# Two pools of six 8 KB tiles in place of one pool of twelve, in a two-layer decoder trunk

## The chip, the cores and the metric

One core of a Trainium2 chip runs the whole kernel. The metric is the device time of one execution in microseconds (us). The engines are named as in the profile: PE (TensorE; PEld are its weight loads), DVE (VectorE), ACT (ScalarE), POOL (GpSimd) and SP (SyncE, which here only issues DMAs). Each engine works through its own queue strictly in the order in which the program was written out for it.

## What is computed

Two layers, each with four sub-layers on x of 512 tokens by 1024 columns, everything in float32. The part that matters here is the SwiGLU, which stands twice in each layer:

```python
def swiglu(x, w_in, w_out):
    gate, up = jnp.split(x @ w_in, 2, axis=-1)
    return (jax.nn.silu(gate) * up) @ w_out

for l in range(DEPTH):                       # DEPTH = 2, D_FF = 2816
    x = x + 0.5 * rms_norm(swiglu(rms_norm(x, ln_ffn1_pre[l]), w_ffn1_in[l], w_ffn1_out[l]), ln_ffn1_post[l])
    x = x + rms_norm(token_mixing(...), ln_mix_post[l])
    x = x + 0.5 * rms_norm(swiglu(rms_norm(x, ln_ffn2_pre[l]), w_ffn2_in[l], w_ffn2_out[l]), ln_ffn2_post[l])
    gate = jax.nn.sigmoid(rms_norm(x, ln_ple_pre[l]) @ w_ple_gate[l])
    x = x + rms_norm(gate * (p[l] @ w_ple_proj[l]), ln_ple_post[l])
```

## The kernel before

**Precision.** A float32 operand is split into a high part (a rounding copy, on ACT, line 139) and a low part (the rest, on DVE or POOL, line 140), and a product is three matmuls: high by high (L167), high by low (L168) and low by high (L169). So each weight tile is loaded by a DMA into a raw tile and must pass through ACT and then DVE before PE can use it.

**A SwiGLU's first half** (`ffn`) is a loop over 22 *units*, one for each block of 128 hidden columns. A unit multiplies by a scheme of seven products instead of eight (block sums of the weights and of x take the place of the eighth); a product is 4 x 3 matmuls of 128x256, so a unit has 84. What a unit needs, in the code's names: the raw weights `wr` (two DMAs of 512 KB, `ffn_load`, L316); the split `w12` of their first half, for the products `gate` starts with (bank `p12`); block sums `sx` and `sy` (DVE, L355, L357, L358) and their splits `w75` and `w63`; and the split `u2` (also printed as `w4`) of a quarter. DVE then puts the banks together (L367, L370, L372, L374, L375, L378), ACT applies silu (L376), and DVE writes the product into the hidden tile `h` (L382). One `h` tile holds four units, so a new one is asked for in units 0, 4, 8, 12, 16 and 20.

**The second half** (`ffn_out`) runs in two passes over the output's halves (h = 0 and 1). A pass takes *P blocks* (plain: 48 matmuls) and *S blocks* (the seven-product scheme, for two hidden blocks at once) in the order of `FSEQ`: P0 S3 S4 P1 S5 S6 P2 S7 S8 S9 in the first pass, S6 S7 S8 S9 S3 S4 S5 in the second. A tail of plain blocks (10 in the first pass; 0, 1, 2 and 10 in the second) is multiplied token block by token block, and after each token block `finish` empties its banks with the help of the tile `us` (DVE, L497). An S block's weights come by DMA into `ws_r` (L440), get three sums on DVE (L442 to L444) and a split `wb`; the hidden tiles get theirs as `hq`, which stay from their P block to the end of the second pass.

**The slots.** All these tiles, and others, are 8 KB per partition, and they come from one pool, `slots`, by `slot()`: one tag, "s", with twelve buffers (`NS`). They are: `xr` (x kept for later sums), three `tx` (sums of x for products 4, 6 and 7, alive for the whole first half), `wr`, `h`, `hq`, `ws_r`, `us`, the splits of the second pass's tail weights, `wor`/`wot` of the mixing's output product, and `pT`/`wpg` of the last sub-layer. The pool is closed during the token mixing and opened again after it.

**What sets the order.** The program is written for a framework that schedules it before it runs: it takes the instructions by the order of the source, gives each tile a buffer of its tag when its turn comes, estimates times, and writes a fixed queue for each engine. Tiles of one tag are given out in the order in which the source asks for them: a tile cannot get a buffer before every tile that was asked for earlier with that tag has been given one, even while buffers are free. In the source, the `h` tile of unit 4 is asked for at the end of unit 4's body, ahead of the `wr` of unit 5. What the scheduler sets is the order in the queues; on the chip an instruction waits only for its own semaphores and for what stands ahead of it in its engine's queue.

Of the kernel before, what the change touches and what calls it, by code (L numbers as in the profile page):

```python
# [9 lines left out]
F32 = mybir.dt.float32  # L10
F32R = mybir.dt.float32r
# [9 lines left out]
NM = DFF // 128  # L21
EPS = 1e-6
SLOT = 2048
NS, NW = 12, 3
G = 4
BANKS = {"m": 2, "r": 3}
MAINL, AUXL = "mmoa", "brrr"
# [45 lines left out]
class Trunk:  # L73
# [35 lines left out]
    def close_slots(self):  # L109
        self.slots_pool.__exit__(None, None, None)  # L110

    def slot(self, shape, name, dt=F32):
        assert np.prod(shape) <= SLOT
        return self.slots.tile([128] + list(shape), dt, tag="s", name=name, bufs=NS)

    def pl_(self, i):
        return self.nc.gpsimd if PL[i] == "1" else self.nc.vector
# [33 lines left out]
    def wblock(self, ap, name, slot=False, raw=None, eng=None):  # L151

        c = ap.shape[1]
        if raw is None:
            raw = self.wraw.tile([128, c], F32, tag="raw", name=name + "_r")
        self.nc.sync.dma_start(out=raw, in_=ap)
        if slot:
            w = self.slot([2, c], name, F32R)
            self.split(w[:, 0], w[:, 1], raw, eng)
            w = w[:, 0], w[:, 1]  # L160
        else:
            w = self.wsplit(raw, name, eng)
        return [self.cut(w, slice(i * c // 2, (i + 1) * c // 2)) for i in range(2)]
# [46 lines left out]
    def turn(self, t, xn, ffn):  # L210
        nc = self.nc
        v_, a_, g_ = nc.vector, nc.scalar, nc.gpsimd
        ps = []
        for j in range(2):
            p = self.aux_tile("xtp").rearrange("p (a b) -> p a b", a=4)
            for i in range(4):
                k = 4 * j + i
                nc.tensor.transpose(p[:, i], xn[:, k * 128:(k + 1) * 128], self.ident)
            ps.append(p)
        kss = [slice(0, 4), slice(4, 8)]  # L220
        ts = slice(t * 128, (t + 1) * 128)
        if ffn and t == 0:
            self.xr = self.slot([2, 8, 128], "xr")
        if ffn and t == 2:
            self.tx = [self.slot([2, 4, 256], "tx", F32R) for _ in range(3)]
        if not ffn or t < 2:
            for p, ks in zip(ps, kss):
                self.split(self.xh[:, ks, ts], self.xl[:, ks, ts], p)
                if ffn:
                    a_.activation(self.xr[:, t, ks], p, AF.Copy)  # L230
            return
        EB, E1, E3, E4 = None, g_, g_, g_

        u = t - 2
        xr = self.xr
        t2, t3 = (self.tmp.tile([128, 4, 128], F32, tag="tb0", name="tx", bufs=4) for _ in range(2))
        t1, t4 = (xr[:, u, ks] for ks in kss)
        a_.activation(t3, ps[0], AF.Copy)
        v_.tensor_tensor(t1, t1, ps[0], ALU.subtract)
        v_.scalar_tensor_tensor(t2, ps[1], -1.0, t1, ALU.mult, ALU.subtract)  # L240
        v_.tensor_tensor(t3, ps[1], t3, ALU.subtract)
        g_.tensor_tensor(t4, t4, t2, ALU.add)
        self.split(self.xh[:, kss[1], ts], self.xl[:, kss[1], ts], ps[1], EB)
        us = slice(u * 128, u * 128 + 128)
        self.split(self.xh[:, kss[0], ts], self.xl[:, kss[0], ts], t1, E1)
        for q, x, e in zip(self.tx, (t2, t3, t4), (None, E3, E4)):
            self.split(q[:, 0, :, us], q[:, 1, :, us], x, e)
# [14 lines left out]
    def out_proj(self, nb, part, blocks, gain, scale, after, tail):  # L262

        half0 = []
        for h in range(2):
            ps = [self.mm_tile("y0") if h == 0 else self.aux_tile("y1") for _ in range(NT)]
            cut = nb - (tail if h else 1)

            def one(i, w, a, t):
                for j in range(2):  # L270
                    self.mm3(ps[t], [q[:, t * 128:(t + 1) * 128] for q in a[j]], w[j],
                             i == 0 and j == 0, i == nb - 1 and j == 1)

            for i in range(cut):
                w, a = self.wblock(blocks(h, i), "wo", eng=self.nc.gpsimd if h == 0 and OW[i] == "1" else None), part(h, i)
                for t in range(NT):
                    one(i, w, a, t)
            raws = [None] * nb
            if h and tail == nb:
                raws = [q[:, j] for q in [self.slot([2, 1024], "wor") for _ in range(nb // 2)] for j in range(2)]  # L280
            rest = [(i, self.wblock(blocks(h, i), "wot", bool(h), raws[i], self.nc.gpsimd if (raws[i] is not None and OE[i] == "1" if h else OW[i] == "1") else None), part(h, i)) for i in range(cut, nb)]
            def finish(t):
                e = self.out_evac(ps[t], gain, h, scale)
                if h == 0:
                    half0.append(e)
                else:
                    self.postnorm(t, half0[t], e, scale)
                    self.late.append(after(t))

            for t in range(NT):  # L290
                for i, w, a in rest:
                    one(i, w, a, t)
                if t:
                    finish(t - 1)
                if h and t > 1:
                    self.flush(1)
            self.ending(h, finish)
# [12 lines left out]
                f()  # L310

    def ffn_load(self, l, w, ms):
        rs = [self.slot([2, 1024], "wr") for m in ms]
        for i in range(2):
            for m, r in zip(ms, rs):
                self.nc.sync.dma_start(out=r[:, i], in_=self.ins[f"w_ffn{w}_in"][l, m, i])  # L316
        return rs
# [6 lines left out]
    def ffn(self, l, w, after):  # L324
# [11 lines left out]
        hs = []  # L336
# [16 lines left out]
        def unit(m, r, pa, a):  # L353
            sx, sy = (self.wraw.tile([128, 1024], F32, tag="raw", name="ws") for _ in range(2))
            v_.tensor_tensor(sx.rearrange("p (i c) -> p i c", i=2), r[:, :, lo],  # L355
                             r[:, 1].rearrange("p (i c) -> p i c", i=2), ALU.add)
            v_.tensor_tensor(sy[:, lo], sx[:, hi], r[:, 0, lo], ALU.add)  # L357
            v_.tensor_tensor(sy[:, hi], sy[:, lo], r[:, 0, hi], ALU.add)  # L358
            sx, sy = self.wsplit(sx, "w75"), self.wsplit(sy, "w63")
            u2 = [self.tmp.tile([128, 512], F32R, tag="sg", name="w4") for _ in range(2)]  # L360
            self.split(u2[0], u2[1], r[:, 1, hi])
            pc, pb, pd = self.aux_tile("p63"), self.aux_tile("p75"), self.mm_tile("p4")
            b = self.tmp.tile([128, S], F32, tag="tb1", name="up", bufs=2)

            P, Q = (L, H) if m % 2 else (H, L)
            product(6, self.cut(sy, lo), pc[:, L])
            v_.tensor_tensor(a[:, Q], pc[:, L], a[:, P], ALU.add)  # L367
            product(7, self.cut(sx, lo), pb[:, P])
            product(5, self.cut(sx, hi), pb[:, Q])
            v_.tensor_tensor(b.rearrange("p (i t) -> p i t", i=2), pb.rearrange("p (i t) -> p i t", i=2),  # L370
                             a[:, None, Q].to_broadcast([128, 2, 256]), ALU.add)
            v_.tensor_tensor(a[:, P], pa[:, H], a[:, P], ALU.add)  # L372
            product(3, self.cut(sy, hi), pc[:, H])
            v_.tensor_tensor(a[:, Q], pc[:, H], b[:, Q], ALU.add)  # L374
            v_.tensor_tensor(b[:, Q], pb[:, Q], b[:, P], ALU.add)  # L375
            a_.activation(a, a, AF.Silu)  # L376
            product(4, u2, pd[:, L])
            v_.tensor_tensor(b[:, P], b[:, P], pd[:, L], ALU.subtract)  # L378
            if m % 4 == 0:
                hs.append(self.slot([8, 256], "h"))  # L380

            v_.scalar_tensor_tensor(hs[m // 4][:, m % 4 * 2:m % 4 * 2 + 2], b.rearrange("p (i t) -> p i t", i=2), -1.0,  # L382
                                    a.rearrange("p (i t) -> p i t", i=2), ALU.mult, ALU.mult)
# [15 lines left out]
    def ffn_out(self, hs, blocks, gain, scale, after):  # L399
# [12 lines left out]
        def plain(h, b, slot=False):  # L412
            w = self.wblock(blocks(h, b), "wo", slot)
            if b not in kept:
                q = self.slot([2, 4, 256], "hq", F32R)
                self.split(q[:, 0], q[:, 1], raw(b))
                kept[b] = q
            return w, kept[b]
# [17 lines left out]

        def right(ap):

            r = self.slot([8, 256], "ws_r")
            nc.sync.dma_start(out=r[:, 0:4].rearrange("p i d -> p (i d)"), in_=ap)  # L440

            v_.tensor_tensor(r[:, 4:6], r[:, 1:4:2], r[:, 0:1].to_broadcast([128, 2, 256]), ALU.add)  # L442
# [7 lines left out]
        for h in range(2):  # L450
# [32 lines left out]
                        for u in range(2):  # L483
                            add(n, u, A[n], B[n], b == sb[-1] and n not in (2, 3, 4))
            rest = [plain(h, b, bool(h)) for b in tail]
            us = self.slot([4, 512], "us")
            u1, u2, u3, u4 = (us[:, i].rearrange("p (u d) -> p u d", u=2) for i in range(4))
            a_.activation(u1, banks[1], AF.Copy)
            v_.tensor_tensor(u2, banks[6], u1, ALU.add)
# [1024 lines left out]
```

## Time and profile before

| | us |
|---|---|
| median of three runs | 2292.49 (2291.95 to 2295.7) |
| the profiled execution, device time | 2293.78 |
| its span in the trace | 2292.1 |
| PE busy | 2154.4 (94%) |
| DVE busy | 1735.3 (76%) |
| ACT busy | 1006.8 (44%) |
| POOL busy | 330.7 (14%) |

The profiled execution took 1.7 us more than its span, and 1.3 us more than the median. The four first halves of the SwiGLUs end, by the trace, near 283, 969, 1420 and 2102 us. In the trace's rows, a wait is given in brackets behind the instruction that came after it, with the instruction that ended it. The start column is in us from the span's start. A matmul's duration overlaps the next one's: the pace of PE is the distance from start to start.

### The profile page before, as it was taken

What the parts mean: (1) busy time and instruction counts of PE and PEld (TensorE: products, weight loads), DVE (VectorE), ACT (ScalarE), POOL (GpSimd) and SP (SyncE); (2) the same over time, 40 slices, a digit from 0 to 9 for tenths busy, and PEclk for the clock granted to TensorE, in tenths of its full rate; (3) what the DMA queues carried; (4) which work ended last, traced back from release to release, by engine and by line L of the source; (5) the groups of instructions that cost most, each with busy time, mean ns of one, the idle gap of its engine ahead of it and who ended that gap; (6) DMA issues with size and microseconds to landing.
All of it is one profiled execution on the core that took longest, in us unless ns stands there. A gap on an engine that the chain in (4) does not pass through costs nothing.

```text
span 2292.1 us, 39759 instructions
## 1 busy us (share of the span) xinstructions
PE 2154.4 (94%) x16256; PEld 1991.3 (87%) x16256; DVE 1735.3 (76%) x2886; ACT 1006.8 (44%) x1653; POOL 330.7 (14%) x424
## 2 busy tenths in 40 slices
PE   5999999999988999999979999999999989999998
PEld 5998999888767998999879899998887789899996
DVE  8988886555768888886688888775557698888774
ACT  4343433446545443433554344344464454344343
POOL 4000001132234000002330000111322330000111
PEclk9999999999999999999989999999999999999999
DMA  5222123322032222123322122243220322122232
GB/s 211 93 74 75 65 83 129 124 74 56 20 146 94 93 74 74 65 83 129 138 111 86 62 84 70 78 142 121 61 60 12 147 111 93 56 92 74 90 115 73
DMA packets 67495, 208.61 MB, mean 91 GB/s; under 512 B 15728, under 2 KB 16752, under 8 KB 67312
## 3 DMA queue, kind: packets, MB, share of 16 engines
q1 hardware_dynamic: 67312, 206.07, 25.5%
q8 instruction: 127, 2.08, 0.4%
q14 instruction: 56, 0.46, 0.1%
HBM read 199.23 MB, written 6.82 MB: 90 GB/s over the span
## 4 chain that ended last, share of the span: by engine, by line
PE 74%; DVE 12%; ACT 5%; DMA 3%; issue 3%; POOL 1%; SPq 0%; ACTq 0%; DVEq 0%; POOLq 0%
PE y L463 14%; PE p L169 12%; PE p L167 12%; PE p L168 12%; DVE w L140 2%; PE pkrv L169 1%; PE pkrv L168 1%; PE pkrv L167 1%; DVE xn L207 1%; PE y L169 1%; PE y L168 1%; PE y L167 1%; ACT w L139 1%; PE pgt L167 1%; PE pgt L168 1%
## 5 line engine op out<-in xcount | busy, mean ns | idle before, releaser
L167 PE MATMUL p<-xh,w 128*128 128x256 f32 x1408 | 415.9, 296 | 50.7 <-ACT w L139 46.3
L169 PE MATMUL p<-xh,w 128*128 128x256 f32 x1408 | 415.5, 295 | 9.8 <-POOL w L140 6.4
L168 PE MATMUL p<-xl,w 128*128 128x256 f32 x1408 | 411.6, 293 | 0.2 <-DVE xl L140 0.2
L167 PEld LDWEIGHTS p<-xh,w 128*128 128x128 f32 x1408 | 283.4, 202 | 57.0 <-ACT w L139 50.4
L167 PE MATMUL p<-tx,w 128*128 128x256 f32 x1056 | 301.3, 289 | 15.5 <-ACT tx L139 11.7
L168 PE MATMUL p<-tx,w 128*128 128x256 f32 x1056 | 296.8, 284 | 6.5 <-DVE tx L140 6.5
L169 PEld LDWEIGHTS p<-xh,w 128*128 128x128 f32 x1408 | 283.5, 201 | 15.1 <-DVE w L140 8.1
L169 PE MATMUL p<-tx,w 128*128 128x256 f32 x1056 | 293.3, 284 | 2.9 <-DVE w L140 2.9
L139 ACT ACTIVATE w<-ws 128x1024 fp32r<-128x1024 f32 x176 | 186.1, 1057 | 244.1 <-PE p L169 139.3
L168 PEld LDWEIGHTS p<-xl,w 128*128 128x128 f32 x1408 | 283.3, 201 | 0.9 <-DVE xl L140 0.8
L140 DVE TENSOR_TENSOR w<-ws,w 128x1024 fp32r<-128x1024 f32 x176 | 221.6, 1259 | 49.9 <-ACT w L139 46.9
L167 PEld LDWEIGHTS p<-tx,w 128*128 128x128 f32 x1056 | 202.8, 192 | 23.7 <-ACT tx L139 13.0
L168 PEld LDWEIGHTS p<-tx,w 128*128 128x128 f32 x1056 | 203.5, 193 | 7.6 <-DVE tx L140 7.6
L169 PEld LDWEIGHTS p<-tx,w 128*128 128x128 f32 x1056 | 199.7, 192 | 3.3 <-DVE w L140 3.2
L499 POOL TENSOR_TENSOR tb<-tb,ln_ffn_post 128x512 f32<-128x512 f32 x16 | 27.2, 1700 | 1192.6 <-ACT junk L196 1192.3
L463 PE MATMUL y<-wo,hq 128*128 128x256 f32 x1536 | 190.5, 282 | 0.0
L463 PEld LDWEIGHTS y<-wo,hq 128*128 128x128 f32 x1536 | 185.2, 190 | 0.4
L139 ACT ACTIVATE w<-wr 128x512 fp32r<-128x512 f32 (+1 forms) x176 | 144.2, 839 | 62.5 <-PE p L169 22.1
L463 PE MATMUL y<-ws_r,h 128*128 128x256 f32 x672 | 158.2, 379 | 0.0
L140 DVE TENSOR_TENSOR w<-wr,w 128x512 fp32r<-128x512 f32 (+1 forms) x161 | 152.4, 947 | 0.8 <-ACT w L139 0.7
L463 PEld LDWEIGHTS y<-ws_r,h 128*128 128x128 f32 x672 | 121.3, 190 | 13.4
L376 ACT ACTIVATE gate<-gate 128x512 f32<-128x512 f32 x88 | 54.9, 624 | 142.5 <-DVE gate L374 142.4
(426 smaller groups left out, 4745.7 us busy)
## 6 DMA issues: line engine op xcount, KB each, us to landing
wr<-in_w_ffn_in SPq DMA_DIRECT2D x176, 512.0 KB, 4.2
ws_r<-in_w_ffn_out SPq DMA_DIRECT2D x56, 512.0 KB, 3.7
wo_r<-in_w_ffn_out SPq DMA_DIRECT2D x32, 512.0 KB, 3.2
pkrv_r<-in_w_rw SPq DMA_DIRECT2D x16, 512.0 KB, 3.7
wpg_r<-in_w_ple_gate SPq DMA_DIRECT2D x16, 512.0 KB, 4.2
xd<-x SPq DMA_DIRECT2D x8, 512.0 KB, 3.1
x<-xd SPq DMA_DIRECT2D x8, 512.0 KB, 3.3
pq_r<-in_w_q SPq DMA_DIRECT2D x8, 512.0 KB, 3.5
```

The lines of the kernel that those rows point to most:

```text
L139: self.nc.scalar.activation(hi, src, AF.Copy)
L140: (eng or self.nc.vector).tensor_tensor(lo, src, hi.bitcast(F32), ALU.subtract)
L167: mm(out, a[0], b[0], start=first, stop=False)
L168: mm(out, a[0], b[1], start=False, stop=False)
L169: mm(out, a[1], b[0], start=False, stop=last)
L207: v_.scalar_tensor_tensor(xn[:, h], self.x[:, t, h], r, gain[:, h], ALU.mult, ALU.mult)
L376: a_.activation(a, a, AF.Silu)
L463: nc.tensor.matmul(banks[n][:, u], x, y, start=n not in seen, stop=last and i == len(todo) - 1, skip_group_check=True)
L499: (g_ if not h or QL[0] == "1" else v_).tensor_tensor(tb, tb, gain[:, h * 512:h * 512 + 512], ALU.mult)
```

## The change

`slot()` gets a tag: "q" or "h", with six buffers each in the same pool, and every caller names one.

```diff
-NS, NW = 12, 3
+NQ, NH, NW = 6, 6, 3
...
-    def slot(self, shape, name, dt=F32):
+    def slot(self, tag, shape, name, dt=F32):
         assert np.prod(shape) <= SLOT
-        return self.slots.tile([128] + list(shape), dt, tag="s", name=name, bufs=NS)
+        return self.slots.tile([128] + list(shape), dt, tag=tag, name=name, bufs={"q": NQ, "h": NH}[tag])
...
-            w = self.slot([2, c], name, F32R)
+            w = self.slot("h", [2, c], name, F32R)
...
-            self.xr = self.slot([2, 8, 128], "xr")
+            self.xr = self.slot("h", [2, 8, 128], "xr")
...
-            self.tx = [self.slot([2, 4, 256], "tx", F32R) for _ in range(3)]
+            self.tx = [self.slot("q", [2, 4, 256], "tx", F32R) for _ in range(3)]
...
-        rs = [self.slot([2, 1024], "wr") for m in ms]
+        rs = [self.slot("h" if m == 3 else "q", [2, 1024], "wr") for m in ms]
...
-                hs.append(self.slot([8, 256], "h"))
+                hs.append(self.slot("h", [8, 256], "h"))
...
-                q = self.slot([2, 4, 256], "hq", F32R)
+                q = self.slot("q", [2, 4, 256], "hq", F32R)
...
-            r = self.slot([8, 256], "ws_r")
+            r = self.slot("q", [8, 256], "ws_r")
...
-            us = self.slot([4, 512], "us")
+            us = self.slot("q", [4, 512], "us")
```

The raw tiles `wor` of the mixing's output product get "q" too. So "h" holds `xr`, the `wr` of unit 3, the hidden tiles and all splits that live in slots; "q" holds the three `tx`, all other `wr`, `hq`, `ws_r`, `wor` and `us`. No arithmetic, no DMA and no instruction is added or removed. But the queues of the engines are written anew, and they change in all SwiGLUs. Three places:

**ACT's queue, units 7 to 9 of the first SwiGLU.** `w_1382` is the `w12` of unit 9, `w_1421` its `u2`, `w_1415` and `w_1418` its `w75` and `w63`; the two `L376` rows are the silu of units 7 and 8 (they stand merged as x2), and `L351` copies a bank. Before:

```order
L139 ACTIVATE w_1294<-ws 128x1024
L351 ACTIVATE gate<-p_1259 128x256
L139 ACTIVATE w_1297<-ws 128x1024
L376 ACTIVATE gate<-gate 128x512 x2
L139 ACTIVATE w_1382<-wr 128x1024
L139 ACTIVATE w_1421<-wr 128x512
L139 ACTIVATE w_1415<-ws 128x1024
```

And now:

```order
L139 ACTIVATE w_1294<-ws 128x1024
L351 ACTIVATE gate<-p_1259 128x256
L139 ACTIVATE w_1297<-ws 128x1024
L139 ACTIVATE w_1421<-wr 128x512
L139 ACTIVATE w_1382<-wr 128x1024
L376 ACTIVATE gate<-gate 128x512
L139 ACTIVATE w_1415<-ws 128x1024
L351 ACTIVATE gate<-p_1380 128x256
```

Unit 9's first splits stood behind the silu of unit 8; now they stand ahead of the silu of unit 7.

**DVE's queue, the same place.** `p_1304`, `p_1305` and `p_1306` are banks of unit 8. Before:

```order
L367 TENSOR_TENSOR gate<-p_1304,gate 128x256
L372 TENSOR_TENSOR gate<-p_1259,gate 128x256
L370 TENSOR_TENSOR up<-p_1305,gate 128x512
L374 TENSOR_TENSOR gate<-p_1304,up 128x256
L375 TENSOR_TENSOR up<-p_1305,up 128x256
L378 TENSOR_TENSOR up<-up,p_1306 128x256
L382 SCALAR_TENSOR_TENSOR h<-up,gate 128x512
L140 TENSOR_TENSOR w_1382<-wr,w_1382 128x1024
L355 TENSOR_TENSOR ws<-wr 128x1024
L140 TENSOR_TENSOR w_1422<-wr,w_1421 128x512
```

And now, where the last two rows are unit 8's first sums of banks and unit 7's `h`:

```order
L374 TENSOR_TENSOR gate<-p_1184,up 128x256
L357 TENSOR_TENSOR ws<-ws,wr 128x512
L375 TENSOR_TENSOR up<-p_1185,up 128x256
L140 TENSOR_TENSOR w_1382<-wr,w_1382 128x1024
L358 TENSOR_TENSOR ws<-ws,wr 128x512
L378 TENSOR_TENSOR up<-up,p_1186 128x256
L140 TENSOR_TENSOR w_1422<-wr,w_1421 128x512
L140 TENSOR_TENSOR w_1415<-ws,w_1415 128x1024
L367 TENSOR_TENSOR gate<-p_1304,gate 128x256
L382 SCALAR_TENSOR_TENSOR h<-up,gate 128x512
```

All of unit 8's bank sums and its `h` stood ahead of unit 9's first split; now the split stands ahead of all of them, among unit 7's bank sums (`p_1184`, `p_1185`, `p_1186`).

**DVE's queue where the second pass of the first SwiGLU's output begins.** `ws_r_3522`, `ws_r_3560` and `ws_r_3598` are the weights of the second pass's S6, S7 and S8; `us_3432` is the first pass's `us`, which the L497 rows of its four token blocks read. Before (eight L497 rows in all, five of them behind these):

```order
L442 TENSOR_TENSOR ws_r_3560<-ws_r_3560 128x512
L490 TENSOR_TENSOR us_3432<-y0_7_2942,us_3432 128x512
L491 TENSOR_TENSOR us_3432<-y0_5_2943,us_3432 128x512
L140 TENSOR_TENSOR wb_3527<-ws_r_3522,wb_3527 128x1024
L497 TENSOR_TENSOR tb_3462<-y0_2_2944,us_3432 128x256
L443 TENSOR_TENSOR ws_r_3560<-ws_r_3560 128x256
L442 TENSOR_TENSOR ws_r_3598<-ws_r_3598 128x512
L492 TENSOR_TENSOR us_3432<-y0_5_2943,us_3432 128x512
L497 TENSOR_TENSOR tb_3462<-y0_3_2945,us_3432 128x256
L497 TENSOR_TENSOR tb_3481<-y0_4_2946,us_3432 128x256
```

And now (the last five of the eight L497 rows, and what follows them):

```order
L497 TENSOR_TENSOR tb_3481<-y0_8_2947,us_3432 128x256
L140 TENSOR_TENSOR wb_3527<-ws_r_3522,wb_3527 128x1024
L497 TENSOR_TENSOR tb_3500<-y0_2_2944,us_3432 128x256
L497 TENSOR_TENSOR tb_3500<-y0_3_2945,us_3432 128x256
L497 TENSOR_TENSOR tb_3507<-y0_4_2946,us_3432 128x256
L497 TENSOR_TENSOR tb_3507<-y0_8_2947,us_3432 128x256
L442 TENSOR_TENSOR ws_r_3560<-ws_r_3560 128x512
L443 TENSOR_TENSOR ws_r_3560<-ws_r_3560 128x256
L444 TENSOR_TENSOR ws_r_3560<-ws_r_3560 128x256
```

The weights of S7 and S8 were there while the first pass was being emptied; now S7's come after its last L497: of the six "q" slots, four hold `hq` tiles until the second pass ends, and S7's `ws_r` takes the slot of `us`.

More of the change, by code (lines that the diff above doesn't have):

```diff
@@ L279, in out_proj @@
             if h and tail == nb:
-                raws = [q[:, j] for q in [self.slot([2, 1024], "wor") for _ in range(nb // 2)] for j in range(2)]
+                raws = [q[:, j] for q in [self.slot("q", [2, 1024], "wor") for _ in range(nb // 2)] for j in range(2)]
             rest = [(i, self.wblock(blocks(h, i), "wot", bool(h), raws[i], self.nc.gpsimd if (raws[i] is not None and OE[i] == "1" if h else OW[i] == "1") else None), part(h, i)) for i in range(cut, nb)]
```

## Prediction

> **What bounds the kernel now.** I read the page first, then PE's waits, then stretches and single rows.
>
> ```profile
> PE 2154.4 (94%) x16256; PEld 1991.3 (87%) x16256; DVE 1735.3 (76%) x2886; ACT 1006.8 (44%) x1653; POOL 330.7 (14%) x424
> PE p L167 <- ACT w L139: 49.6, 32, 3.1
> PE xtp L218 <- DVE xn L207: 19.1, 10, 9.5
> ```
>
> PE is the bound; its longest wait in total (us, times, longest) is for ACT's split of a weight at L167, the first matmul of a product. The stretches below begin where PE starts again after the longest of these waits (columns: stretch, length, busy time of PE, PEld, DVE, ACT and POOL, granted PE clock, DMA share, GB/s).
>
> ```profile
> 90.35:135.02 44.67, 42.29 (x336) 41.66 (x336) 38.65 (x58) 17.92 (x25) 0.00 (x0) 0.96 0.20 72
> 135.02:179.71 44.69, 42.30 (x337) 41.68 (x337) 38.10 (x57) 18.20 (x25) 0.00 (x0) 0.96 0.20 71
> 179.71:224.75 45.04, 42.31 (x337) 41.49 (x337) 38.82 (x58) 18.19 (x25) 0.00 (x0) 0.96 0.25 94
> 224.75:270.57 45.82, 42.48 (x336) 41.62 (x337) 39.34 (x58) 19.14 (x26) 0.00 (x0) 0.95 0.10 36
> ...
> 866.66:911.33 44.67, 42.34 (x337) 41.45 (x337) 38.48 (x58) 18.17 (x25) 0.00 (x0) 0.96 0.25 95
> 1317.10:1361.86 44.76, 42.45 (x336) 41.58 (x336) 38.50 (x58) 18.20 (x25) 0.00 (x0) 0.96 0.26 95
> 1955.09:1999.80 44.71, 42.47 (x337) 41.56 (x337) 38.47 (x58) 18.21 (x25) 0.00 (x0) 0.96 0.19 71
> 101.60:123.90 22.30, 22.30 (x190) 22.30 (x189) 21.12 (x32) 9.94 (x13) 0.00 (x0) 1.00 0.24 83
> 90.35:95.60 5.25, 5.00 (x24) 4.59 (x25) 5.25 (x8) 1.53 (x2) 0.00 (x0) 0.67 0.01 3
> ```
>
> Every stretch of 336 matmuls (four units of 84) takes 44.7 us or a little more, in each of the four SwiGLUs. Inside one, PE runs at 22.30 / 190 = 0.117 us a matmul (the window also counts two or so that straddle its ends, so I take 0.118): a unit could take 9.9 us, four 39.6. So 5.1 us are lost per four units. Where, the rows around 135 us show:
>
> ```profile
> 132.62 0.28 PE L169 MATMUL p<-xh,w 128*128 128x256 f32 x1
> 135.02 0.38 PE L167 MATMUL p<-xh,w 128*128 128x256 f32 x1 [2.13 <-ACT w L139]
> 136.28 0.44 PE L169 MATMUL p<-xh,w 128*128 128x256 f32 x1 [0.23 <-DVE w L140]
> 133.39 0.63 ACT L376 ACTIVATE gate<-gate 128x512 f32<-128x512 f32 x1 [5.47 <-DVE gate L374]
> 133.93 1.56 ACT L139 ACTIVATE w<-wr 128x1024 fp32r<-128x1024 f32 x2
> 132.94 0.42 DVE L374 TENSOR_TENSOR gate<-p,up 128x256 f32<-128x256 f32 x1 [0.72 <-PE p L169]
> 134.38 0.69 DVE L382 SCALAR_TENSOR_TENSOR h<-up,gate 128x512 f32<-128x512 f32 x1
> 135.00 1.23 DVE L140 TENSOR_TENSOR w<-wr,w 128x1024 fp32r<-128x1024 f32 x1
> ```
>
> PE finishes unit 8 and has nothing left. Only then can DVE take L374 and ACT the silu, and unit 9's `w12` is split behind these in both queues. It is the queue and not the transfer:
>
> ```profile
> L316 SPq DMA_DIRECT2D wr<-in_w_ffn_in x6: 327/380/433, 95.7 to 121.0; - x6
> ...
> DMA to landing us min/median/max: 3.3/3.8/4.2
> ```
>
> The last raw weights issued between 90 and 135 us left at 121.0 and had landed by 125.2, ten microseconds before the wait ended. Behind the wait PE also runs slowly: 24 matmuls took the 5.25 us of the last stretch above, at a granted clock of 0.67, in place of 2.8. Waits and slow clock together: 2.13 + 2.4 = 4.5 of the 5.1 us.
>
> The Trainium skill (TensorE: Matmul & The Clock Gate, "What's actually happening") halves the clock only after an idle window of about 3.4 us. Here 2.13 us of idling was enough, so the trace differs; by the rule a stall would cost its idle time alone, and twenty would be worth some 45 us instead of 102.
>
> **The change, part by part.** The order shows unit 9's splits moved from behind unit 8's last sums into unit 7's.
>
> *Stalls that go.* One stands where a new `h` is written before the next `wr` may be placed: before units 5, 9, 13, 17 and 21, so five in each SwiGLU and twenty in all, at 5.1 us: 102 us at most.
>
> *What is late next: DVE.* It is busy 38.65 us per four units, 9.66 a unit, under PE's 9.9. I went through two units of the new queue (168 matmuls, 19.8 us of PE) with the durations of the rows: each split is done at least 1 us before PE's first use of it, and DVE waits twice, some 0.5 us together (for a `w75` whose buffer PE holds, and for the bank of L367), so it needs 20.0 us. That would lose 0.1 us a unit. The other bound is the fast stretch above, in which DVE sat idle 22.30 - 21.12 = 1.18 us in 2.25 units, 0.52 a unit: 9.66 + 0.52 = 10.18, a loss of 0.28. In between I take 0.2, nearer the second, since a queue worked out by hand has no jitter: 88 units x 0.2 = 18 us (9 to 25). The stalls' gain becomes 84 us (77 to 93).
>
> *Raw weights.* In mid-SwiGLU three `wr` slots are left. A slot is freed when unit m's `u2` is split, and its next tile is first read some two units, 20 us, later; a load takes 4.2 at most by the row above. It costs nothing unless a load took five times that.
>
> *The second pass's S7.*
>
> ```profile
> 350.30 0.42 DVE L497 TENSOR_TENSOR tb<-y,us 128x256 f32<-128x256 f32 x1 [1.51 <-PE y L463]
> 354.60 0.69 DVE L442 TENSOR_TENSOR ws_r<-ws_r 128x512 f32<-128x512 f32 x1 [1.99 <-DMA ws_r<-in_w_ffn_out]
> 360.52 2.75 PE L463 MATMUL y<-ws_r,h 128*128 128x256 f32 x12
> 357.46 3.22 PE L463 MATMUL y<-wb,xh 128*128 128x256 f32 x24
> 68.25 0.39 PE L167 MATMUL p<-xh,w 128*128 128x256 f32 x1 [0.92 <-DVE gate L367]
> ```
>
> Before, S9's weights already followed `us`: the L497 that freed it began at 350.30 and they were there at 354.60, 4.3 us later. Now it is S7's. In that time PE has what is left of S6 behind the first pass: 21 of its 24 split matmuls at 3.04 / 24 (2.7 us) and 8 of its 12 others at 2.46 / 12 (1.6), 4.3 in all (the runs of 24 and 12 start at 357.46 and 360.52, and the next at 362.92). A tie; then S7's own sums and split (0.69 + 0.42 + 1.06 + 1.22 = 3.4, of which PE covers 12 x 0.2 = 2.5) come late by some 1 us. SP holds the loads of S8 and S9 behind it, DVE S7's sums; they ride along. I take 1 us at four places: 4 us. At the other end S7 is hidden (0); or the gap reaches the 2.13 that halved the clock and costs as much as a stall, 5.1: 20 us. A gap of 0.92 us, the last row, is followed by matmuls at full pace, so I stay near the low end. Behind S7 two slots alternate: S(k+2) asks 2.5 us into S(k), and has its split 4.3 + 3.4 later, at 10.2, when its turn is at 2 x 5.46 = 10.9. No wait, with 0.7 to spare.
>
> *The last sub-layer.* Of the four `wpg` splits of its first half, three now wait for a slot of the SwiGLU's tail, two before. One more split at 1.22 us then lies on DVE between tail and gate product: 2 x 1.2 = 2 us (0 if PE has projections to do, 6 if a gap follows). SP also issues two `wr` tiles ahead of the fourth `wpg`, which waits for its raw buffer anyway: nothing.
>
> *The starts.* Splits on POOL move among prenorms.
>
> ```profile
> 18.48 5.23 POOL L140 TENSOR_TENSOR w<-wr,w 128x1024 fp32r<-128x1024 f32 x2 [2.17 <-ACT w L139]
> 21.90 4.06 DVE L207 SCALAR_TENSOR_TENSOR xn<-x,r,ln_ffn_pre 128x512 f32<-128x512 f32 x2
> 15.82 1.40 DVE L207 SCALAR_TENSOR_TENSOR xn<-x,r,ln_ffn_pre 128x512 f32<-128x512 f32 x2
> ```
>
> Beside POOL's split the same two DVE instructions took 4.06 instead of 1.40 us. What meets what is dealt anew, so 3 us either way in the first start and as much in the third SwiGLU's: 0, from -6 to +6.
>
> **Sum.** -84 + 4 + 2 + 0 = -78. The profiled execution took 2293.78, 1.3 above the median: 2215.8 on its own footing, **2215** as a median.
>
> **Rivals.** *DVE becomes the bound.* For: 9.66 of 9.9 us, so each hitch counts. Against: the hand pass. If half of DVE's idle time now (44.67 - 38.65 = 6.0 per four units) stays, four units take 41.7 and twenty stalls give 20 x 3.0 = 60; less 6: 2292.5 - 54 = **2238**.
>
> *Too few slots for raw weights (slower).* Twelve slots let four tiles wait; three may not. If each third unit now waited for a load as each fourth waits for a split, there would be 29 stalls for 20: 9 x 5.1 + 6 = 52 more, **2344**. It decides when a load takes 20 us; against it stand the 4.2. This is how the Trainium skill would have it (Perfetto Trace Analysis, "Optimization Strategy": the same gap repeating on the engine that should be saturated can mean that too few buffers are there for the next tile). The trace agrees that the gap repeats, but the weights lay ready.
>
> *The second pass runs on two slots (slower).* If each of its 7 S blocks waited, in four SwiGLUs 28 waits: they eat up the gain from 78 / 28 = 2.8 us each. With only one slot in effect a block takes 10.2 instead of 5.46: 28 x 4.7 = 132, and 2292.5 - 84 + 132 + 2 = **2342**. The 0.7 us to spare is little, but a miss of it would cost tenths.
>
> *No change.* The stalls stay because something else holds unit 9's splits, such as the buffers of `w`: **2292**. Against it the moved rows.
>
> **Chances.** Forecast 0.74, DVE as the bound 0.18, too few raw slots 0.02, two slots in the second pass 0.04, no change 0.02. The forecast's own terms reach from -93 - 6 = -99 (2194) to -77 + 20 + 6 + 6 = -45 (2247); the second case centres at 2238 and its worse half lies above. The range 2195 to 2255 leaves out the slower cases, no change, and the tail of the second. A measurement of this kernel tells 0.2% (4.6 us) from no change: faster 0.92, same 0.02, slower 0.06.
>
> **What would show it.** After: the wait of `p` L167 for ACT falls from 49.6 to under 15 us, and no idle time over 2 us stands inside a first half; four units take 40 to 41 us with the clock at 1.00 and DVE over 93% busy; PE waits about 1 us at S7 four times. If four units take 41.5 or more with PE waiting for DVE's low parts, DVE is the bound; if `w` waits for DMA, the raw slots; if waits stand at each S of the second pass, its slots. Wrong altogether if the 2 us waits at every fourth unit are still there.

## The result, and the profile after

| | before | after |
|---|---|---|
| median of the runs side by side, us | 2294.09 (2291.95 to 2297.81) | **2186.55** (2185.51 to 2188.29) |
| span of the profiled execution | 2292.1 | 2183.8 |

The ratio is 0.953, with an interval from 0.9514 to 0.9547. Three later executions, the first of the kernel with L370 done twice (3446.68 us at a mean granted clock of 0.578) and two of before beside it, ran at a lower clock than the 0.97 to 0.99 of all the others and are left out below. The kernel is 107.5 us faster; the prediction had 78 (2215, from 2195 to 2255), so the direction and the cause were right and the size was not: the time lies 8 us below the range.

The page of after, its first lines:

```profile
span 2183.8 us, 39815 instructions
...
PE 2108.5 (97%) x16256; PEld 1959.2 (90%) x16256; DVE 1718.1 (79%) x2886; ACT 1007.5 (46%) x1653; POOL 330.5 (15%) x424
```

PE's waits in after, the rows that the prediction speaks of (us in total, times, longest):

```profile
PE xtp L218 <- DVE xn L207: 14.9, 7, 9.2
...
PE p L167 <- ACT w L139: 2.0, 6, 0.6
...
PE y L463 <- DVE wb L140: 1.1, 4, 0.3
```

The wait for ACT's split at L167, 49.6 us before, is 2.0 now and never over 0.6. The third row is of S6, the first S block of each second pass. Stretches of after, in each of the four SwiGLUs (columns as in the prediction):

```profile
86.00:125.70 39.70, 39.70 (x336) 39.70 (x336) 37.47 (x58) 18.67 (x26) 0.00 (x0) 1.00 0.30 107
125.70:165.40 39.70, 39.70 (x336) 39.70 (x336) 37.20 (x56) 18.36 (x24) 0.00 (x0) 1.00 0.30 107
165.40:205.10 39.70, 39.70 (x336) 39.70 (x336) 36.80 (x58) 18.08 (x24) 0.00 (x0) 1.00 0.29 107
820.00:859.70 39.70, 39.70 (x336) 39.70 (x335) 37.15 (x56) 18.10 (x25) 0.00 (x0) 1.00 0.29 106
1200.00:1239.70 39.70, 39.70 (x336) 39.70 (x335) 36.88 (x57) 18.02 (x24) 0.00 (x0) 1.00 0.30 112
1900.00:1939.70 39.70, 39.70 (x336) 39.70 (x335) 36.29 (x56) 17.17 (x23) 0.00 (x0) 1.00 0.29 107
```

Four units of 336 matmuls take 39.70 us, with PE busy all the time at full clock. That is PE's own pace, with nothing added by DVE, which is idle 2.2 to 3.4 us in each row.

**Where the 108 us of span went.** I cut both traces into windows of 10 us, added up the matmuls (scaled to equal sums, since one that straddles an edge counts twice), and read off when the same number was done. The distance between the two kernels grows by 25.4, 25.9, 25.8 and 24.1 us in the four first halves: 101.2, or 5.1 for each of the twenty stalls. The other 7.1 us: 2.3 ahead of the first unit; 4.5 between the first two first halves, nearly all of it where the token mixing begins; 0.3 in the rest together. The start of the mixing in layer 0, PE in before and then in after:

```profile
409.83 0.55 PE L167 MATMUL pkv<-pkv,xh 128*128 128x256 f32 x1 [2.30 <-DVE tb L497]
410.18 0.41 PE L168 MATMUL pkv<-pkv,xh 128*128 128x256 f32 x1
```

```profile
380.63 0.36 PE L167 MATMUL pkv<-pkv,xh 128*128 128x256 f32 x1
380.82 0.28 PE L168 MATMUL pkv<-pkv,xh 128*128 128x256 f32 x1
```

A wait of 2.30 us is gone, and the slow matmuls behind it (0.21 us from start to start, against 0.12).

### The profile page after: what moved, and what is told of

Its sections match the earlier page's. It is cut to its first block, busy times and chain, and to the rows that moved or that the text cites. A ratio compares the mean times of both kernels' runs of the same rounds, so it can differ in the third digit from the quotient of the medians.

```text
span 2183.8 us, 39815 instructions
## 1 busy us (share of the span) xinstructions
PE 2108.5 (97%) x16256; PEld 1959.2 (90%) x16256; DVE 1718.1 (79%) x2886; ACT 1007.5 (46%) x1653; POOL 330.5 (15%) x424
## 4 chain that ended last, share of the span: by engine, by line
PE 81%; DVE 9%; ACT 3%; DMA 3%; issue 2%; POOL 2%; SPq 0%; DVEq 0%; POOLq 0%; ACTq 0%
PE y L463 18%; PE p L169 13%; PE p L168 13%; PE p L167 13%; PE pkrv L169 1%; PE pkrv L168 1%; PE pkrv L167 1%; PE y L167 1%; PE y L168 1%; PE y L169 1%; DVE xn L207 1%; DMA ws_r<-in_w_ffn_out 1%; DVE w L140 1%; PE pgt L168 1%; PE pgt L169 1%
## 5 line engine op out<-in xcount | busy, mean ns | idle before, releaser
L169 PE MATMUL p<-xh,w 128*128 128x256 f32 x1408 | 401.1, 286 | 7.5 <-POOL w L140 7.5
L167 PE MATMUL p<-xh,w 128*128 128x256 f32 x1408 | 401.2, 286 | 4.4 <-DVE gate L367 2.4
L168 PE MATMUL p<-xl,w 128*128 128x256 f32 x1408 | 401.1, 285 | 0.4 <-DVE xl L140 0.4
L167 PE MATMUL p<-tx,w 128*128 128x256 f32 x1056 | 295.9, 284 | 9.6 <-ACT tx L139 8.0
L169 PEld LDWEIGHTS p<-xh,w 128*128 128x128 f32 x1408 | 271.9, 193 | 8.1 <-POOL w L140 8.1
L167 PEld LDWEIGHTS p<-xh,w 128*128 128x128 f32 x1408 | 271.7, 194 | 6.7 <-DVE gate L367 3.2
L168 PEld LDWEIGHTS p<-xl,w 128*128 128x128 f32 x1408 | 271.9, 193 | 1.4 <-DVE xl L140 1.3
L167 PEld LDWEIGHTS p<-tx,w 128*128 128x128 f32 x1056 | 201.7, 192 | 12.0 <-ACT tx L139 9.2
L499 POOL TENSOR_TENSOR tb<-tb,ln_ffn_post 128x512 f32<-128x512 f32 x16 | 24.1, 1530 | 1076.5 <-ACT junk L196 1076.5
L351 ACT ACTIVATE gate<-p 128x256 f32<-128x256 f32 x88 | 33.1, 381 | 171.6 <-PE p L169 169.4
```

The costliest lines, as they stand in the source:

```text
L167: mm(out, a[0], b[0], start=first, stop=False)
L168: mm(out, a[0], b[1], start=False, stop=False)
L169: mm(out, a[1], b[0], start=False, stop=last)
L351: a_.activation(a[:, (H, L)[m % 2]], pa[:, L], AF.Copy)
L499: (g_ if not h or QL[0] == "1" else v_).tensor_tensor(tb, tb, gain[:, h * 512:h * 512 + 512], ALU.mult)
```

## The experiments

**The theory.** The gain is the removal of twenty stalls of 5.1 us each, and they came from the order of asking: a `wr` tile stood in one line behind an `h` tile. DVE costs nothing on top because its work in a unit takes 9.3 us of PE's 9.92. **Rivals:** the places count and not the order (more or separate buffers); part of the gain comes from elsewhere; DVE has no room, and something else made up for the 18 us that the prediction took off for it.

### The order of asking alone

One pool of twelve, as before, but each unit's raw weights are asked for earlier in the source:

```diff
+        raws = dict(enumerate(self.ffn_raw))
+        def fetch(m):
+            if m < NM and m not in raws:
+                raws[m] = self.ffn_load(l, w, [m])[0]
...
-            r = self.ffn_raw[m] if m < G else self.ffn_load(l, w, [m])[0]
...
         for m in range(NM):
+            fetch(m + 1)
+            fetch(m + 2)
```

> Before, with one pool of twelve, but each unit's raw weights are asked for one and two units earlier in the source, ahead of the `h` tile that they stood behind. Theory (the stalls come from the order of asking alone: a `wr` tile behind an `h` tile in one line): the twenty stalls go without any second pool, the time is 2187 to 2200 us, and each four units take 39.7 us. Rival (two pools are needed, because with one pool the late tiles of the tail and of the second pass take the places that the raw weights need): at most half of the gain comes, 2240 us or more.

Measured: 2194.18 us, ratio to before 0.957 (0.9551 to 0.959). Two stretches of it, in the first and the third SwiGLU, and its waits at the same places as above:

```profile
127.70:167.40 39.70, 39.70 (x336) 39.70 (x335) 37.39 (x57) 18.23 (x25) 0.00 (x0) 1.00 0.22 80
...
1230.00:1269.70 39.70, 39.70 (x336) 39.63 (x335) 37.41 (x57) 17.92 (x24) 0.00 (x0) 1.00 0.23 81
```

```profile
PE xtp L218 <- DVE xn L207: 18.3, 9, 9.7
...
PE pkv L167 <- DVE tb L503: 3.7, 2, 2.3
```

The stalls are gone with one pool. It stays 7.6 us behind after; by the same count of matmuls 3.3 of its 9.2 us of span are lost in the first halves, most of them at their ends, and 5.9 outside, where it keeps before's waits: 18.3 us at the prenorms' transposes (19.1 before, 14.9 after), and 3.7 at the start of the mixing (0.4 in after). So most of the 7 us outside the first halves go with the new queues that two pools give there, and not with the stalls.

### One place fewer in the one pool

```diff
-NS, NW = 12, 3
+NS, NW = 11, 3
```

> Before with eleven places in the one pool instead of twelve. Theory (the stalls came from the order of asking, and places were not short): within 10 us of before, 2283 to 2303. Rival (the stalls came from a shortage of places, as a gap that repeats may mean): one place less makes more of them, 2320 or more.

Measured: 2296.04 us, ratio 1.0009 (0.9999 to 1.002). PE's wait for ACT's split is nearly what it was (49.6 us in 32 waits):

```profile
PE p L167 <- ACT w L139: 52.2, 34, 3.1
```

Places were not short before: one fewer changes nothing, and the run above removes the stalls with the same twelve. So the order of asking is shown to be the cause. More than twelve places were not run.

### Stalls put back

After, with the raw weights of some units placed behind an `h` tile again, four of the five in each SwiGLU or one:

```diff
-        rs = [self.slot("h" if m == 3 else "q", [2, 1024], "wr") for m in ms]
+        rs = [self.slot("h" if m in (3, 5, 9, 13, 17) else "q", [2, 1024], "wr") for m in ms]   # sixteen in all
+        rs = [self.slot("h" if m in (3, 9) else "q", [2, 1024], "wr") for m in ms]              # four in all
```

> After, with the raw weights of units 5, 9, 13 and 17 placed in the pool of the `h` tiles, behind one: sixteen of the twenty stalls come back and nothing else of the change does. Theory (each stall was worth 5.4 us, the mean of the four periods before less 39.65): 2187 + 16 x 5.4 = 2273 us. By the forecast's own price of 5.1: 2268. Rival (a good part of the gain has another source, such as the two halves of the pool in the second pass): 2250 or less.

> After, with the raw weights of unit 9 alone placed in the pool of the `h` tiles: one stall comes back in each of the four SwiGLUs. Theory (the gain is a sum over stalls): 2187 + 4 x 5.4 = 2208 us, and one period of four units of 45 us in each SwiGLU beside periods of 39.7. Rival (a single stall is caught up by DVE's spare time in the units behind it): 2187 to 2195. Other rival (one stall draws others after it): over 2220.

Measured: 2269.63 us (ratio to before 0.9898, 0.9881 to 0.9915) with sixteen, 2207.08 (0.9622, 0.9608 to 0.9637) with four. Against after's 2186.55 that is 83.1 / 16 = 5.2 and 20.5 / 4 = 5.1 us a stall. With four, the stretch that holds the stall, and the one behind it:

```profile
127.70:167.40 39.70, 38.78 (x308) 38.06 (x309) 37.66 (x53) 18.08 (x24) 0.00 (x0) 0.96 0.22 80
167.40:207.10 39.70, 39.70 (x336) 39.70 (x335) 37.29 (x57) 18.57 (x25) 0.00 (x0) 1.00 0.30 108
```

```profile
128.47 0.39 PE L167 MATMUL p<-xh,w 128*128 128x256 f32 x1 [2.13 <-ACT w L139]
```

In the first row 28 matmuls fewer are done, 3.3 us at 0.118; part of the 2.13 us of waiting lies ahead of the row's start. What follows: the price of a stall in the prediction, 5.1, was right. A stall isn't caught up behind it (the next row is at full pace, no faster), and it draws no other.

The price is not the slow clock's, as the prediction had it (2.4 of the 5.1 us). Behind two of the sixteen stalls the clock stayed at 1.00, and the four units from there took as long as four behind a stall with a slow clock (first row). Then the 5 us behind the first of the two, and its waits:

```profile
134.86:179.55 44.69, 42.43 (x336) 41.57 (x337) 38.50 (x58) 18.22 (x25) 0.00 (x0) 0.96 0.26 95
1938.28:1982.96 44.68, 41.05 (x337) 40.22 (x337) 38.49 (x58) 18.24 (x25) 0.00 (x0) 1.00 0.26 95
1982.96:2027.71 44.75, 41.11 (x337) 40.27 (x337) 38.46 (x58) 18.23 (x25) 0.00 (x0) 1.00 0.26 95
...
1938.28:1943.28 5.00, 4.75 (x35) 4.33 (x36) 5.00 (x7) 1.53 (x2) 0.00 (x0) 1.00 0.00 0
```

```profile
1938.28 0.39 PE L167 MATMUL p<-xh,w 128*128 128x256 f32 x1 [2.13 <-ACT w L139]
...
1944.87 0.39 PE L167 MATMUL p<-tx,w 128*128 128x256 f32 x1 [1.25 <-ACT w L139]
```

At full clock PE does more matmuls at first and then waits again, 1.25 us, for ACT. DVE is busy 5.00 of 5.00 us behind the stall, so I read the price as the work that stands late on DVE and ACT, which PE has to await at either clock; no run tests that reading by itself.

The 5.4 that I took for these runs, from the mean of the four periods before, was too much: the last of those, 45.82 us, ends with the longest wait (3.1), ahead of unit 21, which these runs don't put back.

### How much room DVE has

One instruction of each unit is done twice, so that DVE has more to do. The added time is from start to start, as in these rows of after:

```profile
129.40 1.22 DVE L140 TENSOR_TENSOR w<-ws,w 128x1024 fp32r<-128x1024 f32 x1
130.53 0.69 DVE L140 TENSOR_TENSOR w<-wr,w 128x512 fp32r<-128x512 f32 x1
131.13 0.42 DVE L374 TENSOR_TENSOR gate<-p,up 128x256 f32<-128x256 f32 x1
131.47 0.69 DVE L357 TENSOR_TENSOR ws<-ws,wr 128x512 f32<-128x512 f32 x1
132.06 1.23 DVE L140 TENSOR_TENSOR w<-wr,w 128x1024 fp32r<-128x1024 f32 x1
```

Rows that follow each other without a wait overlap: 1.22 us lasts 1.13 to the next start, 0.69 lasts 0.60, 0.42 lasts 0.34. In the five runs the edit has one form, at different lines:

```diff
-            v_.tensor_tensor(sy[:, lo], sx[:, hi], r[:, 0, lo], ALU.add)
+            for _ in range(2):
+                v_.tensor_tensor(sy[:, lo], sx[:, hi], r[:, 0, lo], ALU.add)
```

The first two, 0.61 us at L370 (bank `p75` into `up`) and 1.14 at L355 (the first weight sum):

> After, with the sum at L370 done twice in each unit: DVE has 0.61 to 0.68 us more a unit, 54 to 60 us in 88 units. Theory (DVE's rows after leave 39.7 - 37.2 = 2.5 us idle per four units, 0.6 a unit, and all of it can be used): 0 to 10 us slower, 2187 to 2197. Rival (the forecast's: a unit of DVE's work needs its busy time and 0.3 to 0.5 us more, so it has no room): 30 to 54 us slower, 2217 to 2241.

> After, with the first weight sum of each unit (L355) done twice: DVE has 1.14 to 1.22 us more a unit, about 104 us in 88 units. Theory (0.6 of it fits into DVE's idle time, and the rest makes DVE the bound): 88 x 0.55 = 48 us slower, 2235. Rival (no room): 100 us slower, 2287. Other rival (DVE's work overlaps PE's waits freely and has far more room than its idle time shows): under 20 us slower.

Measured: 2202.9 us (ratio 0.9608, 0.9591 to 0.9626; the next expectation counts the execution left out too, which makes it 2203.32 and 16.7 us slower) and 2234.03 (0.9747, 0.9731 to 0.9763). With 1.14 the theory's 2235 came out. With 0.61 both missed: 16.4 us slower lies above the theory's 10 and under the rival's 30. I took that for the place of L370, which reads a bank of PE, and moved the same load to L357 (shown above), where weights are summed that PE doesn't wait for at once:

> After, with the weight sum at L357 done twice in each unit: as much more on DVE as in the run before with L370 (0.61 us from start to start), but among the next unit's weights, where no bank of PE waits for it. The run with L370 came out 16.7 us slower than after. Theory (DVE has 0.6 us a unit to spare, and the 16.7 came from the place, since the sum at L370 stands between a bank of PE and its next product): 0 to 6 us slower, 2187 to 2193. Rival (DVE has only some 0.4 us to spare wherever the work stands): 17 us slower, 2203.

Measured: 2220.86 us (0.9695, 0.9678 to 0.9711), 34.3 us slower, twice the cost, where I had expected none. Two stretches, and a wait inside the second with the 5 us behind it:

```profile
120.00:160.00 40.00, 40.00 (x339) 40.00 (x338) 39.32 (x62) 18.44 (x24) 0.00 (x0) 1.00 0.29 106
...
200.00:240.00 40.00, 38.45 (x323) 38.25 (x323) 38.62 (x58) 17.87 (x24) 0.00 (x0) 1.00 0.22 80
```

```profile
216.65 0.39 PE L167 MATMUL p<-tx,w 128*128 128x256 f32 x1 [1.55 <-ACT w L139]
...
215.02 0.63 ACT L139 ACTIVATE w<-wr 128x512 fp32r<-128x512 f32 x1 [2.35 <-PE p L168]
215.56 1.04 ACT L139 ACTIVATE w<-ws 128x1024 fp32r<-128x1024 f32 x1
216.50 1.04 ACT L139 ACTIVATE w<-wr 128x1024 fp32r<-128x1024 f32 x1
```

PE waits 1.55 us in 40, and DVE isn't full (38.62). ACT sits 2.35 us before a split that needs a buffer from PE, with the split that PE needs right behind it (it ends at 216.60): the old kind of stall again, by the order in a queue. The framework writes all queues anew when one instruction is added, and here it wrote worse ones. So this run tells more of an order than of DVE's room, and my reason for it was wrong.

Next, once more L370, for its profile, and two other places: L382, the last of a unit (0.61 us), and L375 (0.34):

> The kernel with the sum at L370 done twice once more, for a profile that can be set beside after. Theory (the place): 2203 us as before, with waits of PE for L367 or L370 or for banks in the first halves while DVE still has idle time. Rival (room): no such waits, DVE busy 39.5 us and more of 40.

> After, with the last instruction of each unit on DVE (L382, the product that writes `h`) done twice, 0.61 us from start to start; nothing in the SwiGLU waits for it. Doubling moves the order on every engine in all these runs. Theory (the load alone costs next to nothing while 9.3 + 0.6 stays under PE's 9.92, and what L357's doubling cost came from the order that it got): 0 to 15 us slower, 2187 to 2202. Rival (0.6 us a unit costs some 34 us where the instruction isn't in PE's way, and L370's place was the lucky one): 2215 or more.

> After, with the sum at L375 done twice in each unit: 0.34 us more on DVE from start to start. Theory (there is room): 0 to 5 us slower, 2187 to 2192. Rival (the forecast's: no room, each microsecond on DVE shows): 30 us slower, 2217. Other rival (the order that comes with any added instruction costs as much as the instruction): 10 us or more.

Measured: L370 again 2203.88 us (0.9614, 0.9599 to 0.9628), L382 2204.75 (0.9613, 0.9587 to 0.9639), L375 2196.32 (0.9575, 0.9556 to 0.9593): 17.3, 18.2 and 9.8 us slower than after, 3 and 5 more than the theory's upper ends for the last two. L375's 9.8 lies at the edge of its other rival, 10 us for the order alone. A stretch with L370 twice, two with L382 twice, and one with L375 twice:

```profile
160.00:200.00 40.00, 40.00 (x334) 39.62 (x333) 39.26 (x61) 18.07 (x23) 0.00 (x0) 1.00 0.27 100
```

```profile
160.00:200.00 40.00, 40.00 (x338) 40.00 (x338) 39.62 (x61) 18.23 (x24) 0.00 (x0) 1.00 0.30 106
...
820.00:860.00 40.00, 40.00 (x334) 39.62 (x333) 39.10 (x61) 18.17 (x24) 0.00 (x0) 1.00 0.28 101
```

```profile
820.00:860.00 40.00, 40.00 (x338) 39.81 (x337) 37.90 (x59) 18.34 (x24) 0.00 (x0) 1.00 0.29 105
```

At PE's full pace 40 us hold 338.5 matmuls. With 0.61 us more a unit there are stretches at that pace with DVE busy 39.62 of 40, and others one per cent under it, in which PE loses its time in bits too short to be listed as waits. The waits of PE that the theory for L370 named do not stand there either: DVE is all but full, nearer the rival. Counted from one matmul to the same matmul in after, units 5 to 21 of the four SwiGLUs together take 9.1 (L370), 9.1 (L382) and 5.8 us (L375) longer in the profiled executions: 0.13, 0.13 and 0.09 a unit. Most of the rest lies in the units ahead of these; what it comes from is open. With 1.14 it is 39.5, 0.58 a unit, near 1.14 - 0.62. So most of the room of 0.6 us is there, with a loss of a tenth of a microsecond a unit as it fills. A DVE without room would have cost all of the added time; up to 0.61 it was about a third of it, but for L357.

### `us` out of the way of S7's weights

```diff
-            us = self.slot("q", [4, 512], "us")
+            us = self.slot("h", [4, 512], "us")
```

> After, with `us` placed in the pool of the `h` tiles, so that the loads of S7 in the second pass no longer wait for a place that `us` holds. Theory (PE waits there 0.3 us at the most, four times): 0 to 2 us faster, 2185 to 2188. Rival (the forecast's: S7 is late by 1 us at four places): 4 us faster, 2183. Other rival (`us` now waits for an `h` tile): slower by 2 us or more.

Measured: 2188.85 us (2187.63 to 2191.17; ratio to before 0.9549, 0.9535 to 0.9563) against after's 0.953 (0.9514 to 0.9547): not faster, perhaps 2 us slower, which the intervals don't tell apart. S7's weights cost after nothing worth removing.

### Five and seven

```diff
-NQ, NH, NW = 6, 6, 3
+NQ, NH, NW = 5, 7, 3
```

> After, with five places in the pool of the raw weights and seven in that of the `h` tiles: two `wr` places are left beside the three `tx` in mid-SwiGLU instead of three. Theory (a load takes 4 us, and a place that comes free is next read some 20 us later with three places and 10 with two, so places are not what binds): 0 to 10 us slower, 2187 to 2197. Rival (the third place is what removed the stalls, and with two the loads come too late, in each unit or every second one): 2250 or more.

Measured: 2248.14 us (0.9807, 0.9791 to 0.9823), 61.6 us slower. Both were wrong on the place; that the time lies near the rival's 2250 is chance. A stretch of the first half, with two `wr` places, and PE's longest waits:

```profile
160.00:200.00 40.00, 40.00 (x339) 40.00 (x338) 36.91 (x57) 17.30 (x23) 0.00 (x0) 1.00 0.29 106
```

```profile
PE y L463 <- DMA ws_r<-in_w_ffn_out: 29.9, 22, 4.1
```

The first halves run at full pace: two raw places are enough there, as the prediction's 4.2 us a load said. The whole loss is in the second passes, 15.7, 14.3, 17.3 and 14.2 us by the count of matmuls. The first S block of such a pass, on DVE, SP and PE, and the 5 us from its wait's end:

```profile
316.46 0.42 DVE L497 TENSOR_TENSOR tb<-y,us 128x256 f32<-128x256 f32 x1 [0.28 <-PE y L463]
316.95 8.17 SPq L440 DMA_DIRECT2D ws_r<-in_w_ffn_out  x2
320.21 0.69 DVE L442 TENSOR_TENSOR ws_r<-ws_r 128x512 f32<-128x512 f32 x1 [3.32 <-DMA ws_r<-in_w_ffn_out]
320.25 4.51 PE L463 MATMUL y<-ws_r,h 128*128 128x256 f32 x12 [3.82 <-DMA ws_r<-in_w_ffn_out]
```

```profile
320.20:325.20 5.00, 4.95 (x18) 4.17 (x19) 2.77 (x4) 1.06 (x1) 0.00 (x0) 0.66 0.00 2
```

Its load leaves right behind the last use of `us`, whose place it needs, and PE waits 3.82 us for it and then runs at a clock of 0.66. With 22 such waits in the four passes, the third rival of the prediction, too few places in the second pass, is real one place further down. It costs less than its price for one slot, 4.7 us for each of 28 blocks or 132: the four passes lose 61.5, 2.2 a block.

No version here beats after.

## Why the prediction was wrong, step by step

- *What bounds the kernel, and the stalls that go* (102 us at most): right. The first halves give 101.2, all twenty stalls are gone, and put back they cost 5.1 and 5.2 each. That an order held the weights, and not a transfer, follows from the prediction's own row (they had landed ten microseconds before the wait ended), and one pool with early asking removes the stalls. Wrong was only what the price is made of: two stalls with the clock at 1.00 cost 5.0 and 5.1, no less than the others.
- *What is late next: DVE* (a loss of 18 us, 9 to 25): this step failed, and it is most of the miss. Nothing was lost: four units take 39.70 us. Of the 30 us between the 78 forecast and the 108 of span, 17 are this term, 6 what was charged to S7 and the last sub-layer, and 7 the gain outside the first halves. It had two faults. The 9.66 us a unit was read in stretches with stalls; in after the same instructions are busy 37.2 / 4 = 9.3 a unit. The sums of the rows' durations are the same in both (41.6 us from 90.35 to 135.02 before, 41.6 from 165.40 to 205.10 after), so what shrinks is the time counted: behind a wait, a row doesn't overlap the one before it. And the idle time of the fast stretch before (0.52 us a unit) was taken as something that DVE needs, although PE was busy 22.30 of 22.30 us there: an engine's idle time beside a full PE is room. The forecast leaned to that bound; its other one, 20.0 us for two units by hand, lies near the 19.85 measured. The added loads bear the room out: 0.6 us fits with a loss of about 0.1 a unit in units 5 to 21, not 0.6.
- *Raw weights* (nothing): right, with more to spare than thought; two places are enough.
- *The second pass's S7* (4 us, 0 to 20): the low end was right, but closely. PE's waits for `wb`, 1.1 us together, are for S6's split, ahead of S7, and `us` in the other pool gains nothing. After, S7's weights are there just as PE comes to them:

```profile
323.12 0.69 DVE L442 TENSOR_TENSOR ws_r<-ws_r 128x512 f32<-128x512 f32 x1 [3.34 <-DMA ws_r<-in_w_ffn_out]
323.07 2.86 PE L463 MATMUL y<-ws_r,h 128*128 128x256 f32 x12
```

- *The last sub-layer* (2 us): not seen. From the end of the last first half to the end of the kernel after loses less than 1 us, which the second pass is part of.
- *The starts* (0, from -6 to +6): the price was from POOL's splits at the prenorms. The gain ahead of the first unit is 2.3 us, within it. The larger gain, at the start of the mixing, had no term at all: I had not gone through the end of the second pass for the first matmuls behind it.
- *The rivals.* DVE as the bound (2238): refuted, 39.70 where it had 41.7. Too few raw slots: refuted. The Trainium skill (Perfetto Trace Analysis, "Optimization Strategy") says that a gap repeating on the engine that should be full can mean too few buffers for the next tile; here it went with twelve buffers when they were asked for in another order, and one fewer changed nothing. The second pass on two slots (2342): refuted for six places, but it was the nearest danger: with five it takes 61.6 us. No change: refuted.
- *The range.* It counted the loss on DVE at 9 us or more in every case. With that term at 0 its fast end would have been 2293.78 - 102 - 6 - 1.3 = 2184.5, and would have held the time, by 2 us and with the unforeseen gain at the mixing in it.

## What to carry to other kernels

When tiles of different lifetimes share one tag, look at which tile each request stands behind; a request that can't be met holds up the later ones even while places are free, and what shows on the chip is a queue in the wrong order, not a late transfer. Read an engine's work per step from rows that run without waits, and count most of its idle time beside a full bound engine as room. Before a pool is split, count the places that every phase needs: here the second pass was the tighter phase, and the first half could have spared a place.

## What the runs showed of the hardware

**The clock.** The granted clock of a stretch is a mean. Three slow stretches in before's first SwiGLU:

```profile
92.11:95.52 3.41, 3.41 (x19) 3.41 (x18) 3.41 (x5) 1.06 (x1) 0.00 (x0) 0.50 0.02 5
136.48:139.89 3.41, 3.41 (x17) 3.41 (x17) 3.41 (x5) 1.06 (x1) 0.00 (x0) 0.50 0.00 0
180.85:184.26 3.41, 2.94 (x13) 2.94 (x14) 3.41 (x5) 1.06 (x1) 0.00 (x0) 0.50 0.00 0
```

Each lasts 3.41 us. They begin 44.37 us apart, 13 times 3.413, while the waits that they follow end 44.67 and 44.69 apart (at 90.35, 135.02 and 179.71): 1.76, 1.46 and 1.14 us behind the wait. The Trainium skill (TensorE: Matmul & The Clock Gate, "What's actually happening") halves PE's clock after an idle window of about 3.4 us and calls that window free-running. The trace agrees with the length and the free running; but no idling of 3.4 us was needed. All twenty waits of 2.12 to 3.07 us between units in before, and fourteen of the sixteen put back, were followed by half the clock within 2.2 us, as here behind the first of the four put back:

```profile
128.47:133.47 5.00, 4.85 (x24) 4.33 (x25) 5.00 (x7) 1.53 (x2) 0.00 (x0) 0.66 0.00 0
```

Waits of up to 1.60 us from 60 us on in the first SwiGLU, with L355 or L357 done twice, never were. The 5 us behind the wait of 1.55 shown above:

```profile
216.65:221.65 5.00, 5.00 (x42) 5.00 (x43) 4.73 (x8) 2.48 (x3) 0.00 (x0) 1.00 0.39 159
```

Nor were waits of 2.17 to 2.54 us near 64 us, with L357, L370 or L382 done twice. So the length of a wait alone doesn't decide, and what does is open.
